# Adds and squared sums of three chunks from VectorE to GpSimd, and a later rank for the last two chunks' post work, in an encoder layer

## The chip, the cores and the metric

The kernel runs on one core of a Trainium2 chip. The core has a matmul engine (TensorE, PE in the profile), three engines for elementwise work (VectorE is DVE, ScalarE is ACT, GpSimd is POOL) and one engine here that issues transfers (SyncE, SP). Each engine works through its own list of instructions in order and waits for others by semaphores; transfers run on 16 DMA engines. The metric is the device time of one execution in microseconds.

## The reference, cut to what matters

One layer of an encoder, 2048 positions of 1024 channels. A mixer (state space model, Fourier mixing and windowed attention side by side) gives `y`, which is projected; then

```python
    x = x + gt_m * rms_norm(y, g_post_mix[l])            # y is the projection
    h = rms_norm(x, g_pre_ffn[l]) * (1.0 + sc_f) + sh_f
    up = dwconv3(h @ w_up[l], conv_w[l], conv_b[l])      # width 3 over positions
    gate, val = jnp.split(up, 2, axis=-1)
    y = (jax.nn.gelu(gate) * val) @ w_down[l]
    x = x + gt_f * rms_norm(y, g_post_ffn[l])
```

The change concerns the first two of these lines.

## The kernel before, in words

Channels lie on the partitions, positions on the free axis. A float32 tile of the kernel's pool holds 2 x 512 values per partition: two channel blocks of a chunk of 512 positions. There are four chunks, 0 to 3.

**Projection.** `proj` takes chunk after chunk. For each it makes 8 output columns of 128 channels, 24 matmuls each (8 blocks of the inner dimension times three, since operands are split into a high and a low float16 part). `proj_evac` copies each column out of PSUM on ACT, squares it there too, and sums the squares on DVE.

**Post work.** For every chunk `proj` starts `post`: load four tiles of the input x; norm 1 (a matmul with ones over the partitions sums the squares, ACT takes the reciprocal root, ACT and DVE refine it); then for each of the four tiles q: multiply by the norm (DVE), add x (L1498, the engine by `POST_E`), store the residual by SP, square it (ACT), and add the squares into one tile (`acc`, L1505). DVE adds the tile's two halves (the half-sum), a second matmul with ones and a second root make norm 2, DVE multiplies the four tiles by it, and ACT applies scale and shift in eight operations (the factors). The result goes to `f_hp[c]`. In chunk 0 the squares are not summed by elementwise work, but by eight ones-matmuls.

**Up-projection.** It runs in two passes p, on chunks 0 and 1 first, then on 2 and 3. `hcomb(p)` makes sums and differences of the two chunks' tiles on DVE (the combination), so that a unit of the up-projection takes seven matrix products, numbered r = 1, 5, 6, 2, 7, 3, 4, in place of eight. A product is 12 matmuls. There are 22 units in a pass. Products leave PSUM through ACT (copies) and DVE (`SCALAR_TENSOR_TENSOR`, a multiply and an add), and product r = 6 adds into the same bank as r = 1, so it waits for ACT's copy of that. Behind a unit's products come the convolution (ACT `Identity`, then two operations on DVE per half), Gelu on ACT and a product on DVE. Weights of each unit are combined on DVE and split into high and low parts.

**What sets the order.** The Python code runs all these as processes under a planner, `Sched`. It keeps a modelled clock for each engine with a modelled cost for each instruction (a POOL sum of 1024 is planned at 0.07 + 0.0022 x 1024 us, on DVE at 0.07 + 0.00105 x 1024), lets the process that can start earliest go next, and gives its instruction the rank

```python
            self.tc.cur_priority = 1000000 + int(PK * (st - p[4]))
```

where `st` is the modelled start and `p[4]` the `ahead` that `spawn` was given. A later scheduler sorts each engine's instructions by that rank as dependencies allow. So an `ahead` of -150 ranks a process 150 modelled microseconds later, and each engine then runs its list in order. Sizes of the pool and counts of PSUM banks (one for the norms' ones-matmuls, `PTAGS["m"]`) are the same in both kernels.

Of the kernel before, what the change touches and what calls it, by code (L numbers as in the profile page):

```python
# [13 lines left out]
ALU = mybir.AluOpType  # L14
# [29 lines left out]
S5_MUL = "V"  # L44
S5_ADD = "V"
G_M1 = 0
POST_B = 0.0
S5_B = 0.0
ATT_B = 0.0
X_AHEAD = (4, 4)  # L50
POST_E = ("VVVV", "VVVV")
ROOM = 2
ATT_GATE = 3
G_FW = 0
# [7 lines left out]
P_POST = 0  # L62
# [140 lines left out]
class Builder:  # L203
# [1208 lines left out]
    def proj(self):  # L1412
        self.x1d = self.dt([P, 8, T], F32)
        self.h2d = self.dt([7, 2, P, 2048], F16)
        for p in range(2):
            self.sc.spawn(self.hcomb(p), 0)
        q = [Fut() for _ in range(32)]
        lead = Sem(3)
        self.sc.spawn(self.wo_stream(q, lead))
        tail = Sem(TAIL)  # L1420
        for c in range(4):
            sl = slice(c * 512, (c + 1) * 512)
            tl = yield ("acq", tail, 1)
            yield ("w", self.f_gm)
            for f in self.f_ya[4 * c:4 * c + 4]:
                ta = yield ("w", f)
            yc = [self.u([2, 2, 512], F16) for _ in range(3)]
            fk = [Fut() for _ in range(5)]
            for k, f in enumerate(self.f_yssm + self.f_yfft):
                self.sc.spawn(self.yc_load(k, tl, f, yc[k // 2][:, k % 2], sl, fk[k]), 1)  # L1430
            ys = [self.u([2, 512]) for _ in range(4)]
            acc = self.u([2, 512])
            fs = [Fut() for _ in range(8)]
            for m in range(8):
                tw = yield ("w", q[8 * c + m])
                w = q[8 * c + m].val
                tb = yield ("acq", self.bank["z"], 1)
                ps = self.ps("z")
                t = max(tb, tw, tl, self.f_gm.t)
                for i, k in enumerate((5, 6, 7, 3, 4, 0, 1, 2)):  # L1440
                    if k < 5:
                        tk = yield ("w", fk[k])
                        r = yc[k // 2][:, k % 2, HI], yc[k // 2][:, k % 2, LO]
                    else:
                        tk = ta
                        r = self.yatt[c][HI][:, k - 5], self.yatt[c][LO][:, k - 5]
                    t = yield from self.mm3(max(t, tk), ps, (w[:, HI, k], w[:, LO, k]), r, i == 0, i == 7)
                lead.give(t)
                if 8 * c + m == self.ATT1:
                    self.f_pj.set(t)  # L1450
                if m == 7:
                    self.f_pc[c].set(t)
                self.sc.spawn(self.proj_evac(t, ps, ys[m // 2][:, m % 2], acc, m, fs))
            self.sc.spawn(self.post(c, fs, ys, acc, tail), P_POST if c else 0, 0.0 if c else POST_B)

    def yc_load(self, k, t, f, dst, sl, done):
        t1 = yield ("w", f)
# [16 lines left out]
    def post(self, c, fs, ys, acc, tail):  # L1474
        A = self.A
        sl = slice(c * 512, (c + 1) * 512)
        yield ("w", self.f_modr)
        xs, tx = [], []

        def load(q):  # L1480
            x = self.u([2, 512])
            tx.append((yield from self.dma(0, x, A["x"][:, 2 * q:2 * q + 2, sl])))
            xs.append(x)

        ahead = X_AHEAD[min(c, 1)]
        for q in range(ahead):
            yield from load(q)
        t = yield ("w", fs[7])
        t = max(f.t for f in fs)
        slack = self.NORM_SLACK if c else 0.0  # L1490
        rt = self.u([2, 512])
        tr = yield from self.rnorm([(max(t, self.f_modr.t), acc[:, 0])], 512, rt[:, 0], rt[:, 1], slack)
        rb = rt[:, 0:1].to_broadcast([P, 2, 512])
        sqs = []
        for q in range(4):
            y, x = ys[q], xs[q]
            t = yield from self.tt(tr, y, y, rb, ALU.mult)
            t = yield from self.tt(max(t, tx[q]), y, y, x, ALU.add, eng=POST_E[min(c, 1)][q])  # L1498
            yield from self.dma(t, self.x1d[:, 2 * q:2 * q + 2, sl], y)
            t = yield from self.act(t, x, y, AF.Square)  # L1500
            if q == 0:
                t = yield from self.ts(t, x[:, 0], x[:, 0], DELTA, None, ALU.add)
                acc = x
            elif c:
                t = yield from self.tt(t, acc, acc, x, ALU.add)  # L1505
            sqs += [(t, x[:, 0]), (t, x[:, 1])]
            if q + ahead < 4:
                yield from load(q + ahead)
        if c:
            t = yield from self.tt(t, acc[:, 0], acc[:, 0], acc[:, 1], ALU.add)  # L1510
            sqs = [(t, acc[:, 0])]
        rt = self.u([2, 512])
        tr = yield from self.rnorm(sqs, 512, rt[:, 0], rt[:, 1], slack)
        fq = []
        for q in range(4):
            t = yield from self.tt(tr, ys[q], ys[q], rt[:, 0:1].to_broadcast([P, 2, 512]), ALU.mult)
            for j in range(2):
                k = 2 * q + j
                t1 = yield from self.act(t, ys[q][:, j], ys[q][:, j], AF.Identity, scale=self.a2[:, k:k + 1],
                                         bias=self.s2[:, k:k + 1])  # L1520
            fq.append(t1)
        tail.give(t1)
        self.f_hp[c].set(t1, (ys, fq))
# [586 lines left out]
```

## Time and profile before

| what | value |
|---|---|
| time, median of 3 runs | 2137.07 us (2134.32 to 2137.93) |
| the profiled execution | 2141.4 us, its span 2139.6 us, granted PE clock 0.962 |
| PE busy | 1963.9 us, 92% of the span |
| DVE busy | 1559.8 us, 73%, 2305 instructions |
| ACT busy | 991.0 us, 46%, 1666 instructions |
| POOL busy | 244.6 us, 11%, 310 instructions |

The span is the time from the first to the last instruction of the execution that was profiled; that execution, 2141.4 us in all, is not among the three timed ones and lies 4.3 us above their median. A row of a timeline has its start, its length (merged rows of one kind with their count, as x4), engine, line, operation, output and inputs by the program's names and shapes, and in brackets the idle time ahead of it on that engine with the engine or the transfer that ended it. A row of a table of groups has busy time and mean nanoseconds of one, then the idle time ahead of them with what ended it. A row of busy time by stage has the stage's bounds in microseconds from the span's start, its length, then busy time with the count for PE, PE's weight loads, DVE, ACT and POOL, then the granted PE clock as a share of full speed, the share of the DMA engines in use and GB/s. Most helper functions record all their instructions at one line: L275 is `tensor_tensor`, L289 `scalar_tensor_tensor`, L282 `tensor_scalar`, L270 any ACT operation, L316 any matmul, L305 `memset`. In the names u is a tile in SBUF, ps one in PSUM, c a constant, d a tile in DRAM.

### The profile page before, as it was taken

What the parts mean: (1) busy time and instruction counts of PE and PEld (TensorE: products, weight loads), DVE (VectorE), ACT (ScalarE), POOL (GpSimd) and SP (SyncE); (2) the same over time, 40 slices, a digit from 0 to 9 for tenths busy, and PEclk for the clock granted to TensorE, in tenths of its full rate; (3) what the DMA queues carried; (4) which work ended last, traced back from release to release, by engine and by line L of the source; (5) the groups of instructions that cost most, each with busy time, mean ns of one, the idle gap of its engine ahead of it and who ended that gap; (6) DMA issues with size and microseconds to landing.
All of it is one profiled execution on the core that took longest, in us unless ns stands there. A gap on an engine that the chain in (4) does not pass through costs nothing.

```text
span 2139.6 us, 26850 instructions
## 1 busy us (share of the span) xinstructions
PE 1963.9 (92%) x9796; PEld 967.3 (45%) x9796; DVE 1559.8 (73%) x2305; ACT 991.0 (46%) x1666; POOL 244.6 (11%) x310
## 2 busy tenths in 40 slices
PE   6788888789988889997999999999999999999997
PEld 1336764444543444443444444444444444434445
DVE  8998898869677767899988875666565763547356
ACT  3643333355566576665555543444444433322221
POOL 1566554002000000000000000000000000011002
PEclk9989999899999989998999999999999999999998
DMA  9362145673746333346655566656565494548533
GB/s 368 105 209 61 56 127 162 217 247 137 256 144 220 126 125 133 136 179 249 223 197 187 188 216 260 230 189 226 201 217 201 158 334 157 162 134 300 177 100 113
DMA packets 206663, 397.27 MB, mean 186 GB/s; under 512 B 19521, under 2 KB 111938, under 8 KB 206530
## 3 DMA queue, kind: packets, MB, share of 16 engines
q1 hardware_dynamic: 206530, 395.55, 53.7%
q8 instruction: 77, 1.26, 0.2%
q14 instruction: 56, 0.46, 0.1%
HBM read 258.93 MB, written 134.98 MB: 184 GB/s over the span
## 4 chain that ended last, share of the span: by engine, by line
PE 49%; DVE 8%; ACT 2%; issue 1%; DMA 1%; POOL 0%; SPq 0%; POOLq 0%; DVEq 0%; ACTq 0%
PE ps L316 49%; DVE u L289 4%; DVE u L275 3%; ACT u L270 2%; DMA u<-d 0%; DMA u<-w_up 0%; DMA d<-u 0%; ACT L270 0%; POOL u L275 0%; SPq L265 0%; POOLq L2095 0%; DVE u L282 0%; ACT c L270 0%; DVEq L289 0%; DVEq L275 0%
## 5 line engine op out<-in xcount | busy, mean ns | idle before, releaser
L316 PE MATMUL ps<-u,u 128*128 128x512 f16 (+5 forms) x9030 | 1879.2, 368 | 90.7 <-DVE u L289 40.5
L316 PEld LDWEIGHTS <-u 128*128 128x128 f16 (+1 forms) x9058 | 846.8, 99 | 1035.4 <-issue 157.6
L275 DVE TENSOR_TENSOR u<-u,u 128x512 f32<-128x512 f32 (+10 forms) x584 | 506.6, 900 | 105.9 <-ACT u L270 92.4
L270 ACT ACTIVATE u<-u 128x1024 f16<-128x1024 f32 (+7 forms) x485 | 406.0, 869 | 360.9 <-DVE u L275 150.3
L270 ACT ACTIVATE u<-ps 128x512 f32<-128x512 f32 (+8 forms) x497 | 268.7, 555 | 410.4 <-PE ps L316 377.5
L289 DVE SCALAR_TENSOR_TENSOR u<-u,c,u 128x1023 f32<-128x1023 f32 (+5 forms) x248 | 291.3, 1197 | 61.2 <-ACT u L270 53.9
L289 DVE SCALAR_TENSOR_TENSOR u<-ps,u 128x512 f32<-128x512 f32 (+4 forms) x231 | 152.3, 666 | 229.2 <-PE ps L316 199.2
L289 DVE SCALAR_TENSOR_TENSOR u<-u,u 128x1024 f16<-128x1024 f32 (+6 forms) x225 | 240.6, 1093 | 61.4 <-ACT u L270 58.1
L275 POOL TENSOR_TENSOR u<-u,u 128x288 f32<-128x288 f32 (+9 forms) x169 | 187.4, 1123 | 609.3 <-DVE u L289 462.4
L270 ACT ACTIVATE u<-u,c 128x1023 f32<-128x1023 f32 (+3 forms) x106 | 123.5, 1166 | 142.5 <-DVE u L289 122.7
L305 POOL MEMSET u<- 128x1 f32 x88 | 8.6, 98 | 1118.0 <-DVE u L289 415.8
L270 ACT ACTIVATE u<-u,st 128x384 f32<-128x384 f32 (+3 forms) x192 | 107.5, 592 | 30.8 <-DVE st L282 17.3
L316 PEld LDWEIGHTS ps<-u,u 128*128 128x128 f32 (+1 forms) x532 | 91.1, 180 | 39.9 <-DVE u L275 16.8
L316 PE MATMUL ps<-u,c 128*128 128x512 f32 (+4 forms) x142 | 61.8, 551 | 43.5 <-DVE u L300 18.5
L316 PE MATMUL ps<-c,u 128*128 128x128 f16 (+1 forms) x568 | 59.6, 229 | 23.9 <-ACT u L270 18.5
L270 ACT ACTIVATE c<-u 128x2 f32<-128x2 f32 (+1 forms) x88 | 17.8, 202 | 132.3 <-DVE u L289 132.2
L275 DVE TENSOR_TENSOR u<-u 128x512 f32<-128x512 f32 (+8 forms) x136 | 67.8, 502 | 12.4 <-ACT u L270 11.6
L300 DVE TENSOR_TENSOR_SCAN u<-u,u 128x512 f32<-128x512 f32 (+1 forms) x60 | 68.6, 1152 | 0.5
L1330 DVE CUSTOM_DVE_ANT_0 u<-ps,u 128x384 f32<-128x384 f32 (+1 forms) x96 | 48.1, 536 | 23.8 <-PE ps L316 23.7
L289 DVE SCALAR_TENSOR_TENSOR u<-u,st,u 128x384 f16<-128x384 f32 (+1 forms) x96 | 54.6, 603 | 12.2 <-ACT u L270 12.0
L270 ACT ACTIVATE u<-u,c,c 128x512 f32<-128x512 f32 (+1 forms) x64 | 48.4, 804 | 22.3 <-DVE u L275 6.2
L316 PEld LDWEIGHTS ps<-u,c 128*128 128x128 f32 (+1 forms) x142 | 23.9, 190 | 72.6 <-issue 46.6
(52 smaller groups left out, 370.9 us busy)
## 6 DMA issues: line engine op xcount, KB each, us to landing
u<-d SPq DMA_DIRECT2D x226, 512.0 KB
d<-u SPq DMA_DIRECT2D x158, 512.0 KB
d<-u SPq DMA_DIRECT2D x111, 256.0 KB
u<-w_ada SPq DMA_DIRECT2D x48, 512.0 KB
u<-w_up SPq DMA_DIRECT2D x44, 512.0 KB
u<-d SPq DMA_DIRECT2D x66, 256.0 KB
u<-x SPq DMA_DIRECT2D x32, 512.0 KB
u<-d SPq DMA_DIRECT2D x24, 511.0 KB
```

Of the source, the lines that this page charges most:

```text
L270: self.S.activation(out, in_, func, **kw)
L275: (self.V if eng == "V" else self.G).tensor_tensor(out, a, b, op)
L289: self.V.scalar_tensor_tensor(out, a, s, b, op0, op1)
L300: self.V.tensor_tensor_scan(out, d0, d1, 0.0, ALU.mult, ALU.add)
L305: (self.V if eng == "V" else self.G).memset(out, v)
L316: self.PE.matmul(o, a, b, start=st, stop=sp, skip_group_check=chain)
L1330: V.tensor_tensor_reduce(out=s_, in0=o, in1=self.bias[h // 2][:, h % 2, bo:bo + nk * 128], op0=ALU.add, op1=ALU.max, scale=1.0, scalar=-3e ...
```

## The change

Four things are changed. `POST_E` for chunks 1 to 3 says G where it said V: the add of x moves from DVE to POOL (4 operations of 128x1024 in each of three chunks). The sum of squares of chunks 1 to 3 moves to POOL (3 of 128x1024 each), which makes 21 in all. `post` of chunks 2 and 3 is given the `ahead` -150, that is a rank 150 modelled microseconds later; `post(0)` and `post(1)` keep 0. The second combination, `hcomb(1)`, gets -150 too. Half-sums, the operation that adds the constant, norms and stores stay as they are. Two more table loads of ACT come in (22 for 20), since its functions alternate differently.

```diff
--- before.py
+++ after.py
@@ -44,11 +44,11 @@
 S5_MUL = "V"
 S5_ADD = "V"
 G_M1 = 0
-POST_B = 0.0
+LATER = (0.0, 0.0, -150.0, -150.0)
 S5_B = 0.0
 ATT_B = 0.0
 X_AHEAD = (4, 4)
-POST_E = ("VVVV", "VVVV")
+POST_E = ("VVVV", "GGGG")
 ROOM = 2
 ATT_GATE = 3
 G_FW = 0
@@ -1413,7 +1413,7 @@
         self.x1d = self.dt([P, 8, T], F32)
         self.h2d = self.dt([7, 2, P, 2048], F16)
         for p in range(2):
-            self.sc.spawn(self.hcomb(p), 0)
+            self.sc.spawn(self.hcomb(p), 0, -150.0 * p)
         q = [Fut() for _ in range(32)]
         lead = Sem(3)
         self.sc.spawn(self.wo_stream(q, lead))
@@ -1451,7 +1451,7 @@
                 if m == 7:
                     self.f_pc[c].set(t)
                 self.sc.spawn(self.proj_evac(t, ps, ys[m // 2][:, m % 2], acc, m, fs))
-            self.sc.spawn(self.post(c, fs, ys, acc, tail), P_POST if c else 0, 0.0 if c else POST_B)
+            self.sc.spawn(self.post(c, fs, ys, acc, tail), P_POST if c else 0, LATER[c])
 
     def yc_load(self, k, t, f, dst, sl, done):
         t1 = yield ("w", f)
@@ -1502,7 +1502,7 @@
                 t = yield from self.ts(t, x[:, 0], x[:, 0], DELTA, None, ALU.add)
                 acc = x
             elif c:
-                t = yield from self.tt(t, acc, acc, x, ALU.add)
+                t = yield from self.tt(t, acc, acc, x, ALU.add, eng="G")
             sqs += [(t, x[:, 0]), (t, x[:, 1])]
             if q + ahead < 4:
                 yield from load(q + ahead)
```

The lists of instructions below are in program order for one engine: line, operation, output and inputs, shape.

POOL in the change, at chunk 3. u_7437 to u_7440 are the chunk's four tiles, u_7765, u_7767, u_7769 and u_7771 its tiles of x, which take the squares afterwards; u_7765 is the sum.

```order
L305 MEMSET u_7877 128x1
L275 TENSOR_TENSOR u_7437<-u_7437,u_7765 128x1024
L275 TENSOR_TENSOR u_7438<-u_7438,u_7767 128x1024
L275 TENSOR_TENSOR u_7439<-u_7439,u_7769 128x1024
L275 TENSOR_TENSOR u_7765<-u_7765,u_7767 128x1024
L275 TENSOR_TENSOR u_7440<-u_7440,u_7771 128x1024
L275 TENSOR_TENSOR u_7765<-u_7765,u_7769 128x1024
L275 TENSOR_TENSOR u_7765<-u_7765,u_7771 128x1024
L305 MEMSET u_8031 128x1
```

Before, these seven were on DVE and POOL had only the memsets here.

DVE before, at the end of chunk 3's sums: u_7424 to u_7427 are the chunk's tiles, u_7786 to u_7792 those of x and the squares, u_7812 the norm; u_7881, u_7882, u_8037 are convolutions of up-projection units 0 and 1, u_7869 and u_7870 evacuated products of unit 1.

```order
L275 TENSOR_TENSOR u_7426<-u_7426,u_7790 128x1024
L289 SCALAR_TENSOR_TENSOR u_7881<-u_7881,u_7882 128x1023
L289 SCALAR_TENSOR_TENSOR u_7869<-ps_7939,u_7869 128x512
L275 TENSOR_TENSOR u_7786<-u_7786,u_7790 128x1024
L275 TENSOR_TENSOR u_7427<-u_7427,u_7812 128x1024
L289 SCALAR_TENSOR_TENSOR u_7870<-ps_7871,u_7870 128x512
L275 TENSOR_TENSOR u_7427<-u_7427,u_7792 128x1024
L289 SCALAR_TENSOR_TENSOR u_7869<-ps_7902,u_7869 128x512
L275 TENSOR_TENSOR u_7786<-u_7786,u_7792 128x1024
L289 SCALAR_TENSOR_TENSOR u_8037<-u_7869,c_1115,u_8037 128x1023
L275 TENSOR_TENSOR u_7786<-u_7786 128x512
L289 SCALAR_TENSOR_TENSOR u_8037<-u_7869,c_1115,u_8037 128x1023
```

DVE in the change, at the same chunk, from norm 1 to the half-sum (u_7787 is the norm, u_8043 unit 1's convolution):

```order
L289 SCALAR_TENSOR_TENSOR u_7787<-ps_7788,u_7787 128x512
L289 SCALAR_TENSOR_TENSOR u_7787<-u_7787 128x512
L275 TENSOR_TENSOR u_7437<-u_7437,u_7787 128x1024
L275 TENSOR_TENSOR u_7438<-u_7438,u_7787 128x1024
L275 TENSOR_TENSOR u_7439<-u_7439,u_7787 128x1024
L282 TENSOR_SCALAR u_7765<-u_7765 128x512
L275 TENSOR_TENSOR u_7440<-u_7440,u_7787 128x1024
L275 TENSOR_TENSOR u_7765<-u_7765 128x512
L289 SCALAR_TENSOR_TENSOR u_8043<-u_7876,c_1115,u_8043 128x1023
L289 SCALAR_TENSOR_TENSOR u_8031<-ps_8102,u_8031 128x512
```

The chunk's products and the half-sum now follow one another; the rows of units 0 and 1 that stood between them stand ahead of the norm or behind the half-sum.

ACT before, at norm 1 of chunk 3 (u_7812) and the first convolution row of unit 0 (u_7881), with u_6650 to u_6653 the tiles of chunk 2 that get their factors:

```order
L270 ACTIVATE u_7812<-ps_7813 128x512
L270 ACTIVATE u_6651<-u_6651,c_367,c_366 128x512 x2
L270 ACTIVATE u_7812<-u_7812 128x512
L270 ACTIVATE u_6652<-u_6652,c_367,c_366 128x512 x2
L270 ACTIVATE u_6653<-u_6653,c_367,c_366 128x512 x2
L270 ACTIVATE c_1116<-u_5496 128x2
L270 ACTIVATE u_7881<-u_5496,c_1115 128x1023
L270 ACTIVATE u_5497<-ps_5498 128x512
L270 ACTIVATE c_1116<-u_5497 128x2
```

ACT in the change, at the same norm (u_7787) and convolution (u_7888):

```order
L270 ACTIVATE c_1116<-u_5497 128x2
L270 ACTIVATE c_1116<-u_5496 128x2
L270 ACTIVATE u_5497<-ps_5498 128x512
L270 ACTIVATE u_7787<-ps_7788 128x512
L270 ACTIVATE u_7888<-u_5496,c_1115 128x1023
L270 ACTIVATE u_7876<-ps_7878 128x512
L270 ACTIVATE u_7889<-u_5497,c_1115 128x1023
L270 ACTIVATE u_7787<-u_7787 128x512
L270 ACTIVATE u_7882<-u_7879 128x1024
```

The root of norm 1 stands ahead of the convolution in both; it now stands behind the last evacuation of unit 0 (u_5497), and chunk 2's factors, which stood around it, are done well ahead of it.

## The prediction

> **What bounds the kernel now.** I read the page first (TensorE, PE, is busy 92% of the span), then the chain of waits, then busy time by stage, then each engine's timeline inside the one stage that matters. In the chain a row is a start, a length and a piece of work; this one is the longest:
>
> ```profile
> 1067.76 634.07 PE ps L316 x2937
> ```
>
> From 1067.8 us on PE runs 634 us in one piece; whatever the change does must be visible at PE before that point, as a later or earlier start of this run. By stage (columns: PE, PE load, DVE, ACT, POOL busy, then the clock granted to PE):
>
> ```profile
> 740.00:767.00 27.00, 12.40 (x61) 6.73 (x59) 23.35 (x39) 17.22 (x35) 0.00 (x0) 0.56 0.33 114
> 840.00:985.00 145.00, 131.84 (x586) 58.38 (x585) 134.51 (x140) 89.50 (x122) 0.99 (x10) 0.95 0.43 158
> 985.00:1068.00 83.00, 78.75 (x362) 35.18 (x361) 78.22 (x86) 52.33 (x75) 1.18 (x12) 1.00 0.64 237
> ```
>
> Chunk 1's post work falls into 740 to 767, where PE is idle for half the time; chunks 2 and 3 fall into 840 to 985. There DVE is busy 134.5 of 145 us, idle 10.5, and feeds PE, which loses 13.2 us. POOL is empty. On PE's own timeline the losses are these (idle time before the row, and what ended it):
>
> ```profile
> 752.22 0.29 PE L316 MATMUL ps<-c,u 128*128 128x128 f16 x1 [11.59 <-ACT u L270]
> ...
> 889.43 1.02 PE L316 MATMUL ps<-u,c 128*128 128x512 f32 x2
> 890.28 5.13 PE L316 MATMUL ps<-u,u 128*128 128x512 f16 x23
> 895.25 1.02 PE L316 MATMUL ps<-u,c 128*128 128x512 f32 x2
> 896.11 15.70 PE L316 MATMUL ps<-u,u 128*128 128x512 f16 x72
> ...
> 931.15 1.13 PE L316 MATMUL ps<-u,c 128*128 128x512 f32 x2
> ...
> 978.77 21.27 PE L316 MATMUL ps<-u,u 128*128 128x512 f16 x84 [10.70 <-DVE u L289]
> ```
>
> The two-matmul f32 rows are ones-matmuls of the norms: 889.43 is norm 2 of chunk 2, 895.25 norm 1 and 931.15 norm 2 of chunk 3. 72 matmuls in 15.7 us make 2.6 us for an up-projection product (12) and 5.2 for a projection column (24). The stage ends with PE waiting 10.7 us for DVE: DVE is behind there, so any DVE delay ahead of 978 arrives at PE in full.
>
> **The parts of the change.** The moved operation has these rows, on DVE today and, for the same shape elsewhere, on POOL:
>
> ```profile
> L275 DVE TENSOR_TENSOR u<-u,u 128x1024 f32<-128x1024 f32 x120 | 146.1, 1234 | 21.9 <-ACT u L270 15.6 <-DMA u<-d 6.3
> L275 POOL TENSOR_TENSOR u<-u,u 128x1024 f32<-128x1024 f32 x2 | 5.3, 2656 | 37.2 <-ACT u L270 31.6 <-issue 5.6
> 24.19 4.99 POOL L275 TENSOR_TENSOR u<-u,u 128x512 f32<-128x512 f32 x4 [12.08 <-issue]
> 60.83 2.37 POOL L275 TENSOR_TENSOR u<-u,u 128x1024 f32<-128x1024 f32 x1 [31.65 <-ACT u L270]
> 83.66 6.67 POOL L275 TENSOR_TENSOR u<-u,u 128x512 f32<-128x512 f32 x4 [4.70 <-DVE u L289]
> ```
>
> On DVE one costs 1.23 us, in a run 1.14 (at 901.49 below three take 3.50, and (3.50 - 1.23) / 2 = 1.14). On POOL it is 2.37 alone; the mean of the two is 2.66; the half shape runs from 1.25 to 1.67, doubled 2.5 to 3.34. I take 2.6 and keep 2.37 and 3.34 as ends. Seven operations per chunk (4 adds of x, 3 adds into the sum of squares) move, so DVE loses 8.0 us of work per chunk and POOL gains 18.2, in one row of seven: behind the first product of a chunk (1.2) the last sum is ready 19.4 us later. Whether that lies beside something is a matter of what stands behind the last product on DVE.
>
> *Chunk 1.* Its adds feed squares on ACT, which stand ahead of the copies that end the 11.59 us gap:
>
> ```profile
> 731.54 1.22 DVE L275 TENSOR_TENSOR u<-u,u 128x1024 f32<-128x1024 f32 x1
> 750.62 1.04 ACT L270 ACTIVATE u<-u 128x1024 f32<-128x1024 f32 x1
> 751.57 0.60 ACT L270 ACTIVATE u<-u,st 128x384 f16<-128x384 f32 x1
> 753.37 0.69 DVE L275 TENSOR_TENSOR u<-u 128x512 f32<-128x512 f32 x1
> ```
>
> From the first product at 731.5 POOL's seven end at 731.5 + 1.2 + 18.2 = 750.9, the half-sum needs them at 753.4, and the fourth square needs only five of them. Cover by the present wait: 2.5 us. I take 0; if POOL's 3.34 held it would be +3, and if DVE's relief brings the exponentials forward, up to -4.
>
> *Chunk 2.* DVE's rows here and in chunk 3:
>
> ```profile
> 840.25 2.35 DVE L275 TENSOR_TENSOR u<-u,u 128x1024 f32<-128x1024 f32 x2
> ...
> 884.68 0.69 DVE L275 TENSOR_TENSOR u<-u 128x512 f32<-128x512 f32 x1
> ...
> 901.49 3.50 DVE L275 TENSOR_TENSOR u<-u,u 128x1024 f32<-128x1024 f32 x3
> ...
> 929.21 1.28 DVE L289 SCALAR_TENSOR_TENSOR u<-u,c,u 128x1023 f32<-128x1023 f32 x1
> 930.41 0.69 DVE L275 TENSOR_TENSOR u<-u 128x512 f32<-128x512 f32 x1
> ...
> 977.42 1.89 DVE L289 SCALAR_TENSOR_TENSOR u<-ps,u 128x512 f32<-128x512 f32 x3
> ```
>
> 840.25 is the start of the combination of chunks 0 and 1, 884.68 and 930.41 the half-sums of chunks 2 and 3, 901.49 chunk 3's first products, 929.21 the first convolution row of up-projection unit 1, 977.42 the evacuations that release PE at 978.77. In the new order some 23 us of rows stand between 840.25 and chunk 2's first product, less what moves ahead of 840: about 861. Half-sum at 861 + 19.4 = 880, with only other products and 2 us of small rows to cover it: DVE idles 12.5 us. That is not late for PE: 880 is ahead of 884.7. What is late next is ACT's eight factors of chunk 2, which stand ahead of the first evacuations of unit 0: PE's third product of that unit, which now stands behind the last projection column, waits from 892 to about 898, and five products (898 + 5 x 2.6) end the unit at 911, not 901 (896.11 and two products); two products of unit 1 are done early for it. DVE, with only evacuations of that unit left, idles some 11 us more.
>
> *Chunk 3, norm 1.* ACT's prices here are these:
>
> ```profile
> L270 ACT ACTIVATE u<-ps 128x512 f32<-128x512 f32 x299 | 175.6, 592 | 208.2 <-PE ps L316 176.7 <-PE ps L899 13.7 <-issue 7.6
> L270 ACT ACTIVATE u<-u,c 128x1023 f32<-128x1023 f32 x44 | 54.1, 1232 | 0.6
> L270 ACT ACT_TABLE_LOAD x20 | 25.7, 1283 | 3.4 <-DMA u<-d 2.3 <-PEq L2092 0.7
> ```
>
> In both orders the reciprocal root stands on ACT ahead of unit 0's first convolution row. But its ones-matmul, at 895.25 today, two products ahead of that unit's end, stands on PE behind the unit and four more products now: 911 + 4 x 2.6 + 1.0 = 922.4, ACT 0.6 more. ACT, in order, holds the convolution until 923.6 and DVE gets its first operand at 924.8, idle for 15 us from 909.7. Then 15.4 us of DVE rows and 2 of waits: chunk 3's first product at 942.3 against 901.5 now.
>
> *Chunk 3, sums.* Nothing stands on DVE between the last product and the half-sum: it waits for POOL's seven, 942.3 + 19.4 = 961.7, idle 14 us (19.4 less four products, 4.6, and a small row). Behind it: PE (waiting at the ones-matmul from about 951), ACT's root 0.6, and unit 1's convolution, which on ACT stands behind that root (1.0 + 0.6 + 1.2 with the 0.3 of gaps): 964.8 against 929.2, **+35.6**.
>
> *From there.* The new order has 39.5 us of DVE rows from that convolution to the evacuation that lets PE go on (today 977.42 + 1.2 - 929.21 = 49.4, of which the combination of chunks 2 and 3 and chunk 3's tail are now placed otherwise): 1004.3 against 978.6, +25.7, and PE has then done 360 product matmuls, not 372: +2.6. **Sum +28.3.** The same by idle time: new waits 12.5 + 11 + 15 + 14 = 52.5, less today's idle 10.5, less 14 x 1.14 = 16.0 moved off, gives +26. Some 6 us of deferred DVE work may delay PE again before its long run: 0 to +6, taken as 0.
>
> *At no cost.* The second combination's later rank: its results are read by the second pass of the up-projection, 22 units of seven products or 22 x 7 x 2.6 = 400 us later; without that cover it is 14 sums of DVE. Two more table loads of ACT (1.28 us each) fall in its waits. On SP the stores of chunk 2's residual now wait for POOL and stand ahead of the last weight loads of the projection; those land at about 880, ahead of the columns that use them; with 3.34 per sum they land 5 later, still ahead of 887.
>
> *A rule against it.* DVE and POOL together show this (the first row groups DVE's operations of that size over the kernel):
>
> ```profile
> L289 DVE SCALAR_TENSOR_TENSOR u<-u,u 128x512 f32<-128x512 f32 x15 | 10.2, 686 | 4.1 <-ACT u L270 3.9
> 68.76 6.88 DVE L289 SCALAR_TENSOR_TENSOR u<-u,c,u 128x512 f32<-128x512 f32 x4
> 75.55 2.28 DVE L275 TENSOR_TENSOR u<-u,u 128x1024 f32<-128x1024 f32 x1
> 68.78 10.18 POOL L275 TENSOR_TENSOR u<-u,u 128x1024 f32<-128x1024 f32 x5 [5.58 <-issue]
> ```
>
> Four DVE rows of 128x512 took 1.72 us each, not the 0.69 of a like operation elsewhere, while POOL's five went on beside them: the two engines seem to take turns. The Trainium skill ("SBUF — State Buffer", section "SBUF: two separate sides") calls their common port an exclusive lock, held for a whole instruction, for DVE operations with two SBUF inputs. These rows agree with it.
>
> **The rivals.** (a) *Waits partly covered.* PE runs other products while chunk 3's sum is waited for, and the ACT hold of 13 to 15 us does not come because PE passes the ones-matmul earlier. For it: an off-path ACT today (89.5 of 145 busy). Against: all engines run in order. Price 28 - 13 = +15, down to +5 with the sums half covered: 2142 to 2152. (b) *Taking turns only.* DVE always finds other rows, but each POOL operation holds it 2.6 instead of 1.14: 14 x 1.46 = +20, about 2157. Against: with DVE idle beside POOL nobody is held. (c) *Relief.* DVE is the bound from 840 on and 14 x 1.14 = 16 us leave it. If POOL's chain ends before DVE has done its other work, PE gets 8 (chunk 3 alone) to 16 us back of its losses (13.2 + 4.3 us in the last two stages): 2121 to 2129. It decides where DVE holds at least 13 us of other rows behind each chunk's last product; the new order holds none. (d) *Nothing.* The late rank keeps both chunks off the path: 2137. Against: unit 0 and unit 1 queue behind their rows. That the change did not do what it says is excluded: the order shows the 21 rows on POOL.
>
> **How the numbers follow.** The profiled execution took 2141.4 us, 1.8 of it outside its span, and lies 4.3 above the median of the runs. 2141.4 + 28.3 = 2169.7, less 4.3: **2165**. Ends: POOL at 3.34 adds 7 x 0.74 = 5.2 per chunk, 10, and the deferred work 6, together 2181; without the ACT hold 2152. Chances: the forecast 0.54 (2152 to 2182), (a) 0.18, (b) 0.10, (c) 0.11, (d) 0.07. The range 2142 to 2182 takes in (a) and (b) and leaves out (c), (d). Within 0.2% (4 us) is what a measurement of this kernel can hardly tell from no change. Slower 0.82, same 0.07, faster 0.11.
>
> **What would show it.** POOL with 21 more 128x1024 sums of 2.4 to 2.9 us, in rows of seven; DVE idle for some 12 us by POOL near 866 to 880 and 14 near 948 to 962; ACT held near 912 to 923 by PE; PE idle by DVE ahead of chunk 3's second ones-matmul; unit 1's convolution near 965; PE's long run beginning near 1095; the 752 gap as before. I am wrong if DVE stays above 90% busy from 840 to 985, or if the half-sums come no later than POOL's fifth sum while PE never waits.

## The result, and the profile after

The changed kernel takes 2190.15 us (median of 4 runs, 2187.1 to 2191.0) against 2135.86 us of the kernel before on the same chip: a ratio of 1.0247, interval 1.0233 to 1.0261. By that ratio it is some 53 us slower (the two medians lie 54.3 apart); the forecast was 28. The direction and the waits named for chunk 3 were right, the size was not, and three steps of the sum were wrong.

From the changed kernel's chain of waits, the row that answers to the 634 us one of before:

```profile
1137.44 616.59 PE ps L316 x2856
```

PE's long run starts at 1137.4 instead of 1067.8, and has 81 matmuls fewer left to do, which is 17.5 us of the difference; 52.2 remain. Busy time by stage, with the bounds that answer to those shown of before:

```profile
740.00:767.00 27.00, 10.01 (x53) 5.28 (x53) 18.79 (x26) 14.61 (x30) 14.34 (x6) 0.62 0.31 107
840.00:985.00 145.00, 111.06 (x483) 48.23 (x484) 88.44 (x89) 67.66 (x100) 38.33 (x20) 0.88 0.28 97
985.00:1137.00 152.00, 132.38 (x581) 57.84 (x579) 140.94 (x152) 90.34 (x128) 1.77 (x18) 0.94 0.59 216
```

Between 840 and 985 DVE falls from 134.5 to 88.4 us of work and PE from 131.8 to 111.1: both wait. POOL takes 38.3. On POOL's timeline and in its groups the moved operations stand like this:

```profile
734.13 2.36 POOL L275 TENSOR_TENSOR u<-u,u 128x1024 f32<-128x1024 f32 x1 [209.65 <-DMA d<-u]
739.30 2.35 POOL L275 TENSOR_TENSOR u<-u,u 128x1024 f32<-128x1024 f32 x1 [2.82 <-DVE u L275]
742.95 10.43 POOL L275 TENSOR_TENSOR u<-u,u 128x1024 f32<-128x1024 f32 x4 [1.31 <-ACT u L270]
754.55 2.35 POOL L275 TENSOR_TENSOR u<-u,u 128x1024 f32<-128x1024 f32 x1 [1.17 <-ACT u L270]
...
957.12 19.32 POOL L275 TENSOR_TENSOR u<-u,u 128x1024 f32<-128x1024 f32 x7 [51.00 <-DVE u L275]
```

```profile
L275 POOL TENSOR_TENSOR u<-u,u 128x1024 f32<-128x1024 f32 x23 | 60.6, 2652 | 421.0 <-DMA d<-u 209.6 <-ACT u L270 151.7 <-DVE u L275 53.8
```

Chunk 3's seven ran as one row of 19.3 us. On PE's timeline the losses are now:

```profile
755.03 0.29 PE L316 MATMUL ps<-c,u 128*128 128x128 f16 x1 [13.53 <-ACT u L270]
...
843.20 0.23 PE L316 MATMUL ps<-c,u 128*128 128x128 f16 x1 [3.42 <-ACT u L270]
...
912.51 25.00 PE L316 MATMUL ps<-u,u 128*128 128x512 f16 x106 [6.13 <-ACT u L270]
937.35 1.02 PE L316 MATMUL ps<-u,c 128*128 128x512 f32 x2
...
977.22 2.07 PE L316 MATMUL ps<-u,c 128*128 128x512 f32 x2 [15.38 <-DVE u L275]
...
1008.64 4.44 PE L316 MATMUL ps<-u,u 128*128 128x512 f16 x12 [6.65 <-ACT u L270]
1017.98 20.51 PE L316 MATMUL ps<-u,u 128*128 128x512 f16 x84 [4.90 <-ACT u L270]
1043.12 9.45 PE L316 MATMUL ps<-u,u 128*128 128x512 f16 x36 [4.64 <-ACT u L270]
```

937.35 is norm 1 of chunk 3, with no idle time ahead of it: PE came to it busy with products, and so it came late (895.25 before). 977.22 is that chunk's norm 2 (931.15 before), for which PE waited 15.4 us. On DVE's timeline:

```profile
847.04 1.22 DVE L275 TENSOR_TENSOR u<-u,u 128x1024 f32<-128x1024 f32 x1
...
876.94 3.38 DVE L275 TENSOR_TENSOR u<-u,u 128x1024 f32<-128x1024 f32 x1
...
893.21 0.69 DVE L275 TENSOR_TENSOR u<-u 128x512 f32<-128x512 f32 x1 [9.28 <-POOL u L275]
...
940.23 1.28 DVE L289 SCALAR_TENSOR_TENSOR u<-u,c,u 128x1023 f32<-128x1023 f32 x1 [14.87 <-ACT u L270]
...
955.81 5.65 DVE L275 TENSOR_TENSOR u<-u,u 128x1024 f32<-128x1024 f32 x3
961.50 2.45 DVE L282 TENSOR_SCALAR u<-u 128x512 f32<-128x512 f32 x1
963.86 3.37 DVE L275 TENSOR_TENSOR u<-u,u 128x1024 f32<-128x1024 f32 x1
976.47 0.69 DVE L275 TENSOR_TENSOR u<-u 128x512 f32<-128x512 f32 x1 [9.24 <-POOL u L305]
981.09 1.28 DVE L289 SCALAR_TENSOR_TENSOR u<-u,c,u 128x1023 f32<-128x1023 f32 x1 [3.92 <-ACT u L270]
```

On ACT, the root of that norm 1:

```profile
938.41 0.60 ACT L270 ACTIVATE u<-ps 128x512 f32<-128x512 f32 x1 [10.62 <-PE ps L316]
```

847.04 is the first combination (840.25 before), 893.21 and 976.47 the half-sums that wait for POOL, 940.23 the convolution of unit 0 behind ACT's hold, 981.09 that of unit 1 (929.21 before). Rows of 1.22 beside POOL's take 3.38, and a small one of 0.43 takes 2.45. PE's last three waits are all for ACT, and ACT's rows ahead of them are these:

```profile
997.92 5.75 ACT L270 ACTIVATE u<-u,c,c 128x512 f32<-128x512 f32 x8 [0.91 <-DVE u L275]
...
1015.26 1.06 ACT L270 ACTIVATE u<-u 128x1024 f16<-128x1024 f32 x1 [6.67 <-DMA u<-w_up]
...
1041.53 1.06 ACT L270 ACTIVATE u<-u 128x1024 f16<-128x1024 f32 x1 [5.48 <-DMA u<-w_up]
```

The first is chunk 3's eight factors in one row (in the kernel before they stand in four pairs from 944.62 on, and PE's longest wait there is 0.65). The other two split weights and wait for their load; in the kernel's chain of waits the loads stand like this:

```profile
1009.02 6.16 DMA u<-w_up
...
1036.11 5.32 DMA u<-w_up
```

In the kernel before no ACT row waits for such a load between 978 and 1075.

### The profile page after: what moved, and what is told of

Read it like the earlier page. It is cut to its first block, busy times and chain, and to the rows that moved or that the text cites. A ratio compares the mean times of both kernels' runs of the same rounds, so it can differ in the third digit from the quotient of the medians.

```text
span 2189.0 us, 26875 instructions
## 1 busy us (share of the span) xinstructions
PE 1976.4 (90%) x9796; PEld 970.3 (44%) x9796; DVE 1557.2 (71%) x2284; ACT 994.1 (45%) x1668; POOL 297.4 (14%) x331
## 4 chain that ended last, share of the span: by engine, by line
PE 62%; DVE 22%; ACT 5%; issue 4%; DMA 4%; POOL 2%; SPq 1%; DVEq 0%; POOLq 0%; ACTq 0%
PE ps L316 62%; DVE u L275 9%; DVE u L289 9%; ACT u L270 5%; POOL u L275 2%; DVE u L300 1%; SPq L265 1%; DMA u<-w_up 1%; DMA d<-u 1%; DMA u<-d 1%; DVE u L1330 1%; DVE u L282 1%; DVE u L444 0%; DVE u L408 0%; DMA u<-w_in 0%
## 5 line engine op out<-in xcount | busy, mean ns | idle before, releaser
L316 PE MATMUL ps<-u,u 128*128 128x512 f16 (+6 forms) x9030 | 1887.9, 369 | 107.4 <-ACT u L270 47.4
L316 PEld LDWEIGHTS <-u 128*128 128x128 f16 (+1 forms) x9058 | 849.9, 100 | 1065.3 <-issue 183.7
L275 DVE TENSOR_TENSOR u<-u,u 128x512 f32<-128x512 f32 (+9 forms) x563 | 492.9, 909 | 104.3 <-ACT u L270 92.8
L275 POOL TENSOR_TENSOR u<-u,u 128x288 f32<-128x288 f32 (+10 forms) x190 | 241.5, 1286 | 993.0 <-DVE u L289 463.3
L316 PE MATMUL ps<-u,c 128*128 128x512 f32 (+4 forms) x142 | 63.4, 564 | 58.5 <-DVE u L275 21.6
L316 PEld LDWEIGHTS ps<-u,u 128*128 128x128 f32 (+1 forms) x532 | 91.3, 181 | 41.8 <-DVE u L275 18.9
L316 PE MATMUL ps<-c,u 128*128 128x128 f16 (+1 forms) x568 | 60.2, 231 | 29.1 <-ACT u L270 23.0
L270 ACT ACTIVATE c<-u 128x1 f32<-128x1 f32 (+1 forms) x88 | 17.9, 203 | 138.7 <-DVE u L289 138.7
L289 DVE SCALAR_TENSOR_TENSOR u<-u,st,u 128x384 f16<-128x384 f32 (+1 forms) x96 | 56.0, 620 | 13.1 <-ACT u L270 12.8
L316 PEld LDWEIGHTS ps<-u,c 128*128 128x128 f32 (+1 forms) x142 | 23.9, 189 | 87.7 <-issue 46.5
```

Source lines behind the costliest of these rows:

```text
L270: self.S.activation(out, in_, func, **kw)
L275: (self.V if eng == "V" else self.G).tensor_tensor(out, a, b, op)
L289: self.V.scalar_tensor_tensor(out, a, s, b, op0, op1)
L316: self.PE.matmul(o, a, b, start=st, stop=sp, skip_group_check=chain)
```

## The experiments

The theory after the result: two prices. One is of the later ranks: a norm's ones-matmul goes behind unit products on PE, while its root stays ahead of the units' rows on ACT, so ACT, and DVE behind it, are held until PE has passed those products. The other is of POOL: chains of seven that are waited for, and DVE rows that are stretched beside them. The rivals: the new order alone, whatever runs on POOL; and turn-taking alone (DVE and POOL holding each other up). Each run stands beside the kernel before as it was timed with it; those medians lie between 2135.9 and 2138.8 us, so a difference between runs of different groups is good to a few microseconds.

| run | what | median, us | before, us | ratio (95% interval) |
|---|---|---|---|---|
| e1_tiny | the change, POOL sums of 16 columns | 2165.10 | 2136.84 | 1.0139 (1.0118 to 1.0161) |
| e2_half | the change, POOL sums of 512 columns | 2173.05 | 2136.84 | 1.0165 (1.0139 to 1.0191) |
| e3_on_dve | the change's plan, sums issued on DVE | 2172.97 | 2136.84 | 1.0176 (1.0154 to 1.0197) |
| e4_rank | later ranks alone | 2156.88 | 2136.84 | 1.0094 (1.0074 to 1.0114) |
| e5_pool | POOL alone | 2168.90 | 2138.77 | 1.0142 (1.0127 to 1.0157) |
| e6_hcomb | later second combination alone | 2132.58 | 2138.77 | 0.9970 (0.9960 to 0.9980) |
| e7_split | the change, rank later only behind norm 1 | 2174.81 | 2138.77 | 1.0177 (1.0150 to 1.0205) |
| e8_pool_c1 | POOL for chunk 1 alone | 2151.81 | 2138.77 | 1.0065 (1.0048 to 1.0082) |
| e9_rank15 | ranks, posts by 15 instead of 150 | 2143.34 | 2136.97 | 1.0031 (1.0021 to 1.0041) |
| e10_rank_p3 | ranks, post of chunk 3 only | 2151.39 | 2136.97 | 1.0074 (1.0054 to 1.0093) |
| e11_hcomb400 | second combination later by 400 | 2131.43 | 2136.97 | 0.9975 (0.9963 to 0.9986) |
| e12_c23 | the change, chunk 1's sums on DVE | 2174.35 | 2136.97 | 1.0180 (1.0158 to 1.0201) |

**POOL's time with the order kept: e1, e2, e3.** In `post` both moved sums call a method that plans them as POOL work with POOL's cost, and issues

```diff
-        self.G.tensor_tensor(out, a, b, op)
+        self.G.tensor_tensor(out[:, 0, 0:16], a[:, 0, 0:16], b[:, 0, 0:16], op)   # e1
+        self.G.tensor_tensor(out[:, 0], a[:, 0], b[:, 0], op)                     # e2
+        self.V.tensor_tensor(out, a, b, op)                                       # e3
```

These lines add five to the kernel, so in rows of e1 to e3 L316 is L321, and L280 is the new method's operation.

> The change with its order of instructions kept on every engine but for a few rows, and each of the 21 POOL sums cut to 16 of its 1024 columns (the rest of the add and of the sum of squares is left out). POOL then costs next to nothing, DVE still has the 24 us less. Theory (POOL's sums are waited for in rows of seven): in the changed kernel's trace DVE waits 9.3 and 9.2 us for POOL, and its rows beside POOL are stretched by 12.8 us in chunks 2 and 3 (each about 2.15 too long) and some 7 in chunk 1; without them 2190 - 31 - 5 = about 2154, the rest being the new order. Rival, taking turns alone: only the stretched rows go, about 2170. Rival, the new order alone does it: 2180 or more.

> The change with exactly its order, each of the 21 POOL sums on 512 of 1024 columns (half of the add and of the sum of squares is left out). Theory: each chain of seven becomes 7 x 1.25 = 8.8 us shorter; two chains on the path and a part of the first, 2190 - 20 = about 2170, halfway between the change and the run with 16 columns. Taking turns alone: about 2180. Order alone: no difference, 2187 to 2191.

> The change's plan (the 21 sums planned as POOL work with POOL's cost, the later ranks), but the sums issued on DVE: nearly the change's order, no POOL work, 24 us of work back on DVE. Theory: the waits and stretched rows (31 and 5 us) go, 16 us of DVE work in the stage where DVE is behind comes back, 2190 - 36 + 16 = about 2170, of which what lies above 2136 is the price of the order. Rival, order alone: 2185 or more. Rival, POOL alone with the order free: 2136 to 2145.

Measured: 2165, 2173 and 2173. So POOL's time is worth 25 us (2190 less 2165), most of it in the second half of its length (8 from 16 to 512 columns, 17 from there to 1024), and the order that came with it 28, although in e1 DVE has 24 us less to do. My account of e1 (2154) was 11 too low; 2165 lies nearer to the 2170 of turn-taking alone. e2 and e3 came near the theory's 2170. e3 has nearly the change's order and all of DVE's work, so its 36 us are the price of that order: 16 more than the later ranks alone cost (e4 below, 20). Planning the sums as POOL work thus makes the order dearer even where POOL does none of them, and POOL in place of DVE adds 17. e1's timelines of DVE and PE show where POOL's 25 went:

```profile
835.99 1.21 DVE L275 TENSOR_TENSOR u<-u,u 128x1024 f32<-128x1024 f32 x1
...
870.69 0.69 DVE L275 TENSOR_TENSOR u<-u 128x512 f32<-128x512 f32 x1 [3.13 <-POOL u L280]
884.20 2.36 DVE L275 TENSOR_TENSOR u<-u,u 128x1024 f16<-128x1024 f32 x2 [12.81 <-ACT u L270]
```

```profile
951.94 1.65 PE L321 MATMUL ps<-u,c 128*128 128x512 f32 x2 [2.31 <-DVE u L275]
...
982.92 4.52 PE L321 MATMUL ps<-u,u 128*128 128x512 f16 x12 [6.65 <-ACT u L270]
992.05 20.69 PE L321 MATMUL ps<-u,u 128*128 128x512 f16 x84 [4.61 <-ACT u L270]
1017.57 9.45 PE L321 MATMUL ps<-u,u 128*128 128x512 f16 x36 [4.83 <-ACT u L270]
```

Chunk 2's half-sum is 22 us earlier than in the change, and DVE then waits 12.8 us for ACT instead of 9.3 for POOL: the wait only changes its name. Of the two waits for POOL only chunk 3's was on the path: at norm 2 PE waits 2.31 us in e1 (951.94) and 15.38 in the change, 13 that turn-taking alone does not explain. In e1 the first combination starts at 835.99, 11 us ahead of the change; 2.4 of these are there where PE's gap ahead of 752 begins, and traces of one order differ by as much there. So 9 to 11 of POOL's 25 us were lost with chunk 1 already. The three last rows are the change's three waits for ACT (6.65, 4.90 and 4.64), and DVE's wait behind norm 1 is 14.87 us in both. They stay with next to no POOL work, and in e3 with none, so they come from the order.

**The ranks alone: e4, e6, e9, e10, e11.** Sums on DVE, and

```diff
-LATER = (0.0, 0.0, 0.0, 0.0)             # e6, e11: the posts' ranks as before
+LATER = (0.0, 0.0, -150.0, -150.0)       # e4
+LATER = (0.0, 0.0, -15.0, -15.0)         # e9
+LATER = (0.0, 0.0, 0.0, -150.0)          # e10
-            self.sc.spawn(self.hcomb(p), 0)
+            self.sc.spawn(self.hcomb(p), 0, -150.0 * p)   # e4, e6, e9, e10; -400.0 * p in e11
```

> One part alone: the later ranks of the posts of chunks 2 and 3 and of the second combination, all sums on DVE as before. The order differs from before in some 60 rows of DVE and 40 of ACT, all after chunk 2. Theory: no chain of seven on another engine, so chunk 3's rows only change places with those of units 0 and 1: 2130 to 2145. Rival, the rank is what is late: 2160 or more.

> One part alone: the second combination's later rank, all else as before. PE's order is the same to the row, 28 rows of DVE change places. Theory: its results are read 400 us later, DVE gets to unit rows earlier: 2128 to 2138. Rival, it is part of the 20 us of the run with all ranks: 2145 or more.

> Ranks alone with one size changed: the posts of chunks 2 and 3 only 15 modelled us later, not 150 (the second combination keeps -150; sums on DVE). Chunk 3's norm-1 ones-matmul stands on PE behind two and a half products past unit 0 in this order, in the run with ranks of -150 behind six, in before two products ahead of unit 0's end. Theory (ACT is held until PE has passed those products, at 2.6 us each, and DVE with it): the hold falls from 19.6 us to 6 to 10, and the 24 us that the posts' ranks cost (2156.9 against the 2132.6 of the combination's rank alone) to 5 to 12: 2137 to 2145. Rival, any rank that breaks the old interleaving costs the same: 2152 or more.

> Ranks alone, only the post of chunk 3 later by 150 (and the second combination); chunk 2's stays. Chunk 2's norm 2 keeps its place, chunk 3's norm 1 stands behind six products past unit 0. Theory: most of the hold is there, since it is chunk 3's norm 1 that ACT is held by: 2146 to 2156. Rival, chunk 2's lateness is what costs: 2130 to 2140.

> The second combination's rank alone, 400 later in place of 150, all else as before. Its work is DVE work of a stage in which DVE is behind, and its results are read 400 us later. Theory: a further few us of DVE work leave that stage: 2126 to 2133. Rival, all of it had left already: 2132 to 2136.

In e4 the norms held back are chunk 2's norm 2 and chunk 3's norm 1, which now follow each other on PE behind the products; in e10 only the latter. The ranks alone cost 20.0 us, more than the theory had of them (2130 to 2145), and not as much as its rival. The second combination's part of them gains 6.2; so the posts' ranks cost 26. e4's ACT timeline shows a part of the price:

```profile
913.67 0.60 ACT L270 ACTIVATE u<-ps 128x512 f32<-128x512 f32 x1 [15.80 <-PE ps L316]
```

and so does DVE's in e4, e10 and e9, at the row that follows the hold:

```profile
914.96 0.69 DVE L289 SCALAR_TENSOR_TENSOR u<-ps,u 128x512 f32<-128x512 f32 x1 [19.59 <-ACT u L270]
```

```profile
916.21 1.28 DVE L289 SCALAR_TENSOR_TENSOR u<-u,c,u 128x1023 f32<-128x1023 f32 x1 [18.59 <-ACT u L270]
```

```profile
902.70 0.69 DVE L289 SCALAR_TENSOR_TENSOR u<-ps,u 128x512 f32<-128x512 f32 x1 [5.34 <-ACT u L270]
```

Waits of 19.6, 18.6 and 5.3 us (3.5 with the combination's rank alone, as in before) go with 2156.9, 2151.4 and 2143.3 us (2132.6). The hold grows with the number of products that the order puts ahead of the ones-matmuls, and the time grows too, but not in step: from e6 to e9 the wait grows by 1.9 us and the time by 10.8 (e9's hold was forecast as 6 to 10; its time, like e10's, lies in its forecast). e9 has a second hold, further on, here on PE and then on ACT:

```profile
966.49 0.61 PE L316 MATMUL ps<-u,u 128*128 128x512 f16 x1 [9.10 <-ACT u L270]
```

```profile
958.79 5.75 ACT L270 ACTIVATE u<-u,c,c 128x512 f32<-128x512 f32 x8
```

Chunk 3's eight factors stand in one row on ACT, and the weight splits that PE waits for stand behind them. e4 and e10, with the factors in a two and a six, have this wait with 9.23 us, e6 none above 3.4. So the ranks cost two holds of ACT, by the norms' roots and by the factors; no run parts the two prices. A rank of 400 for the combination (2131.4) does what 150 does: against its own before it gains 5.5, e6 6.2, although 2131.4 lies in the theory's range. That all of its work had left the stage fits this.

**Where the rank begins: e7.** `post` is cut in two behind norm 1; the first process keeps rank 0.

```diff
+        self.sc.spawn(self.post_sum(c, ys, xs, tx, rt, tr, load, ahead, slack, tail), P_POST if c else 0, LATER[c])
+
+    def post_sum(self, c, ys, xs, tx, rt, tr, load, ahead, slack, tail):
```

> The change, but the later rank begins behind norm 1 of each chunk (the post is cut in two processes, the first keeps rank 0): chunk 3's norm-1 ones-matmul stands on PE ahead of unit 0's last products again, and 15 rows of units 0 and 1 (17 us) stand on DVE between chunk 3's last product and its half-sum. Theory: ACT's hold of 14.9 us goes and the second chain of seven is covered; what stays is the stretching of DVE rows beside POOL and chunk 2's chain: 2135 to 2155. Rival, stretched rows are the price: above 2160. Rival, lateness of norm 2 itself (its ones-matmul stands behind ten products more than in before): 2165 or more.

2174.8: 15 us better than the change, and far outside the theory's range. The ranges of both rivals take it in, and the trace shows both: a hold at norm 2, and stretched rows. ACT, then DVE:

```profile
961.34 0.60 ACT L270 ACTIVATE u<-ps 128x512 f32<-128x512 f32 x1 [10.83 <-PE ps L316]
```

```profile
922.00 7.86 DVE L289 SCALAR_TENSOR_TENSOR u<-u,c,u 128x1023 f32<-128x1023 f32 x3
...
963.10 1.28 DVE L289 SCALAR_TENSOR_TENSOR u<-u,c,u 128x1023 f32<-128x1023 f32 x1 [17.86 <-ACT u L270]
```

The hold did not go, it moved from norm 1 to norm 2: now that one's ones-matmul stands behind the products, its root ahead of unit 1's convolution, and DVE waits 17.9 us. No DVE row waits for POOL in chunk 3 any more, since 15 others stand ahead of the half-sum, but three of 1.28 took 7.86.

**POOL alone: e5, e8, and e12.** No later ranks in e5 and e8; in e8 and e12 the engine depends on the chunk:

```diff
-            t = yield from self.tt(max(t, tx[q]), y, y, x, ALU.add, eng=POST_E[min(c, 1)][q])
+            t = yield from self.tt(max(t, tx[q]), y, y, x, ALU.add, eng="G" if c == 1 else "V")   # e8; c > 1 in e12
-                t = yield from self.tt(t, acc, acc, x, ALU.add, eng="G")
+                t = yield from self.tt(t, acc, acc, x, ALU.add, eng="G" if c == 1 else "V")   # e8; c > 1 in e12
```

> One part alone: the 21 sums on POOL, no later rank. In this order chunk 3's norm-1 ones-matmul stands right behind chunk 2's half-sum on PE (in the change and in the run with ranks alone it stands behind seven or eight products), and 11 rows of the first combination stand on DVE between chunk 2's last product and its factors. Theory (two prices: ACT held by the late norm 1, and chains of seven not covered): no hold, chunk 2's chain covered, chunk 3's not (two small rows behind its last product, some 9 us of wait and 6 of stretched rows), less relief: 2140 to 2155. Rival, the two parts add up: 2190 - 20 = 2170. Rival, the POOL plan's order is dear by itself (the run with 16 columns at 2165): 2165 or more.

> Chunk 1's seven sums alone on POOL, no later rank. Theory: in the changed kernel PE had lost 7 us by the start of the first combination (847.0 against 840.3), of which the POOL chain ahead of the exponentials is the cause; so 2139 to 2146, less what the relief of DVE gives. Rival, relief: 2128 to 2133.

> The change with chunk 1's seven sums back on DVE, everything else (POOL for chunks 2 and 3, ranks) as in the change. Theory, the prices add: 2190 less the 13 us of chunk 1 alone: 2173 to 2181. Rival, by the change's own trace only 7 us were lost by the start of the first combination: 2182 to 2186. Rival, a loss ahead of 840 is taken up by waits behind it: 2187 or more.

POOL alone costs 30.1 us, which with the ranks' 20.0 makes 50: the parts nearly add up, as e5's first rival had it, and my 2140 to 2155 was wrong. 2168.9 lies in the range of the second rival too (the POOL plan's order is dear by itself), and the 16 us between e3 and e4 speak for it. How e5's 30 divide between that order and POOL's time was not run. Its chunk 2 was to be the covered case, with the first combination's sums behind its products. e5's DVE and POOL there:

```profile
854.70 20.88 DVE L275 TENSOR_TENSOR u<-u,u 128x1024 f32<-128x1024 f32 x9
```

```profile
854.44 15.51 POOL L275 TENSOR_TENSOR u<-u,u 128x1024 f32<-128x1024 f32 x5 [2.35 <-ACT u L270]
...
918.73 19.37 POOL L275 TENSOR_TENSOR u<-u,u 128x1024 f32<-128x1024 f32 x7 [25.63 <-DVE u L275]
```

The first POOL row is chunk 2's, the second chunk 3's. Nine DVE rows took 20.9 us, which at 1.14 each are 10.3; POOL's five beside them took 3.1 each instead of 2.36. Moving seven sums saved DVE 8.0 us and the neighbours lost 10.6. So cover does not make it free.

Chunk 1 alone costs 13.0 us, outside both forecasts for e8 (2139 to 2146, 2128 to 2133), and taking it out of the change gives 15.8 back (2190.15 against 2174.35, in e12's forecast): additive again, roughly. But e12's order is not quite the change's: DVE waits 19.58 us behind norm 1, as in e4, and not 14.87, so the 15.8 are not POOL's time alone. The place of e8's loss is not the gap at 752 alone, which grew by 1.9 us. Busy time from 820 to 860, the last attention block, in e8 and in before:

```profile
820.00:860.00 40.00, 25.76 (x139) 13.35 (x138) 32.64 (x60) 26.84 (x51) 0.00 (x0) 0.74 0.47 164
```

```profile
820.00:860.00 40.00, 36.67 (x209) 18.37 (x208) 31.73 (x52) 29.51 (x54) 0.00 (x0) 0.96 0.44 152
```

PE does 10.9 us less there, with POOL idle. In e8's order chunk 2's products and the first combination's sums stand between that block's DVE rows, and PE's rows there wait for DVE and ACT. That POOL is idle in this stretch points to the order in e8; which of its rows did it was not tried. e1, where chunk 1's loss is gone with the change's order kept, shows that in the change it was POOL's time.

**A version that is faster.** e6 and e11 beat the kernel before by 0.3% and 0.25% (intervals above): the one part of the change that has a cover of 400 us and moves nothing to another engine.

## Why the prediction was wrong in size

Point by point, in the order of its own steps.

- **What bounds the kernel, and the sign.** Right. Unit 1's convolution came 51.9 us late on DVE, and PE's long run 52.2.
- **Price on POOL, 2.6 us; a chain of 19.4 us.** Right: 2.652 on the mean of 23, and 19.32 for chunk 3's seven.
- **Chunk 1, taken as 0 with -4 to +3.** This step failed first: 13.0 us alone (e8), 15.8 within the change (e12), each with an order of its own. POOL's seven did not run in 18.2 us but from 734.1 to 756.9, since POOL waited in turn for DVE and ACT (2.82, 1.31 and 1.17 us), and the step looked at the gap at 752 only, not at the attention block behind it. PE lost 3.4 us more at 843.20, in that block, and by the first combination's start the change was 6.8 us late (0.9 of it from ahead of PE's gap).
- **Chunk 2.** The first product was forecast for 861 and came at 871.9, the half-sum for 880 and came at 893.2; of these 13.2 us 6.8 were chunk 1's, some 4 came ahead of the first product (24.9 us behind the first combination's start, not 20.8) and 1.9 in the sums (21.3, not 19.4). "Not late for PE" cost 2.3 us there. The wait of PE's third product (6 forecast, 6.13 at 912.51) was right.
- **Chunk 3, norm 1.** Right: DVE 15 us forecast, 14.87 measured; ACT held, 10.6 us at 938.41. (922.4 and ACT's 0.6 make 923.0 and not the 923.6 of the sum.) e1 and e3 have the same 14.87, so it is of the order; e4, e9 and e10 show that it grows with the rank.
- **Chunk 3, sums.** Right in kind: the chain 19.3, PE idle 15.4 (some 11 forecast, from 951 to 961.7). Unit 1's convolution came 51.9 us late, not 35.6; of the 16.3 missing, 13 had been there at chunk 2's half-sum. The sum also left out the half-sum's own 0.7, and took 1.0 for a ones-matmul that took 2.07.
- **From there, and 0 of 0 to +6 for deferred DVE work.** This step had the wrong limit. It counted DVE's rows and made 28.3 out of the 35.6 at unit 1's convolution, that is 7.3 made up; measured, nothing was: 51.9 there, 52.2 at PE's long run. PE waited for ACT, 6.65, 4.90 and 4.64 us from 1008 on: ACT had chunk 3's factors, and weight splits that waited for their loads, ahead of the evacuations that PE needed. e1 shows that this comes from the order; what holds the loads up was not tried. Before, the longest wait behind the single 10.70 was this:

```profile
1001.88 10.10 PE L316 MATMUL ps<-u,u 128*128 128x512 f16 x46 [1.84 <-DVE u L289]
```

- **Turn-taking (rival b).** "With DVE idle beside POOL nobody is held" failed. In chunks 2 and 3 six rows beside POOL were each some 2.1 us too long (3.38 for 1.22, 2.45 for 0.43), 12.8 together, on top of the waits: b and the forecast were not alternatives but came together.
- **Relief (rival c).** Its point of decision, 13 us of other rows behind the last product, does not suffice: with such rows e5's chunk 2 lost 10.6 us of DVE time for the 8.0 saved.
- **The second combination's rank at no cost.** Better than that: alone it gains 6.2 us (e6).

Added up, 28.3 forecast, 6.8 from chunk 1, 6.4 more by chunk 2's half-sum, 3.1 until unit 1's convolution and 7.6 behind it (the 7.3 not made up and 0.3) make the 52.2 by which PE's long run is late.

## What to carry to other kernels

A later rank acts on each engine's list apart: where it moves a matmul behind other products and leaves its reader on another in-order engine ahead of other work, that engine stands still for all of those products (19.6 us in e4). Look for what the moved part itself puts in one row ahead of others, too, like the eight factors. Seven sums that went from DVE to POOL cost DVE more than they saved where DVE had two-input work beside them (10.6 us for 8.0 in e5), and a chain of 2.6 us steps where it had none; both must be in the sum. So must the order that a planner makes of the new costs: e3 paid 16 us more than e4 for it. And when a moved part touches an early stage, follow it to the next stage's start, not only to the gap beside it.

## What the runs showed of the hardware

In chunks 2 and 3 a POOL operation stretched nearly every DVE row beside it that reads SBUF alone, one-input ones too: the `TENSOR_SCALAR` of 128x512 took 2.45 us instead of 0.43. A row that reads PSUM did not suffer: in e5, with POOL at work from 918.73 to 938.10 (the row above), the first of these took its usual time, the second, with both inputs in SBUF, not its 1.22:

```profile
919.70 0.68 DVE L289 SCALAR_TENSOR_TENSOR u<-ps,u 128x512 f32<-128x512 f32 x1
920.30 2.77 DVE L275 TENSOR_TENSOR u<-u,u 128x1024 f32<-128x1024 f32 x1
```

The Trainium skill ("SBUF — State Buffer", section "SBUF: two separate sides") has it so for the common port: a lock for the whole instruction, against DVE operations with two SBUF inputs or in a two-port mode. The two-input rows and the PSUM row agree; of the one-input row the trace does not say in which mode it ran, only that it was held. POOL is held in turn: 3.1 us for 2.36 beside DVE rows in e5.
